# A hybrid attention block on one core: smaller spinning matmuls, and the first value weights' second half on another queue

## The chip, the cores and the metric

The kernel runs on one core of a Trainium2 chip. The metric is the device time of one execution in microseconds (us), lower is better. The core's engines are TensorE (PE in the profile; PEld are its weight loads), VectorE (DVE), ScalarE (ACT), GpSimd (POOL) and SyncE (SP). Each engine runs its instructions in the order in which they were written for it and waits for others at semaphores. Transfers between main memory and the on-chip buffers are DMAs; SP, ACT and POOL can issue them, each on a queue of its own.

## The reference: what is computed

One encoder layer over 1024 tokens of width 1024. A combined projection gives queries, keys, values and gates for two groups of heads; both groups attend, are gated with SiLU, are joined and projected, and a LayerNorm follows the residual:

```python
h = jnp.einsum('bsd,de->bse', x, w_in[layer])
q_a, k_a, v_a, z_a, q_b, k_b, v_b, z_b = jnp.split(h, SPLIT_POINTS, axis=-1)
y_a = neighborhood_attention(q_a, k_a, v_a, rel_pos_bias[layer])      # 8 heads, 8 x 16 window on a 16 x 64 grid
y_b = windowed_gqa_with_sink(rotary(q_b), rotary(k_b), v_b, sink)     # 8 query heads, 2 key heads, |i - j| <= 128
mixed = jnp.concatenate([y_a * jax.nn.silu(z_a), y_b * jax.nn.silu(z_b)], axis=-1)
x = layer_norm(DEEPNORM_ALPHA * x + jnp.einsum('bse,ed->bsd', mixed, w_out[layer]), ln_gain, ln_bias)
```

(The reshapes into heads are left out.) Inputs and output are float32.

## The kernel before, in words

Matrix products are made more precise by splitting each operand into a high and a low part and running three passes: high by high, low by high, high by low. The kernel has four stages.

1. *Values.* The 640 value columns of both groups (512 and 128) are computed first. The contraction over 1024 is cut into 8 pieces, k = 0 to 7. For the first 512 tokens, each k gives 24 matmuls of 320 columns (line 430): 4 token tiles, 2 halves of the columns, 3 passes, accumulated in 8 banks. For k = 0 alone the passes are the outer loop, so that 4 matmuls need only the first 320 columns of the weights (`wvh`, high part), the next 4 the second 320, then 8 need the low part of x and 8 the low part of the weights (`wvl`). From k = 1 on all three passes run for one tile before the next. Then the second 512 tokens follow, bank by bank.
2. *Projections* of the other columns (line 356, tiles `xf`, `wh`, `wl`) in float16, of which 15 are woven into stage 3. Before them the absolute maxima of x (`x_max`, line 439, on DVE) are gathered, turned by a TensorE transpose in `x_scale` (line 453, with the identity matrix that GpSimd makes at the start) and used to scale x.
3. *Attention* in units of 128 queries: scores (lines 709, 710), minimum and exponential, transposes by DMA, weighted values (line 774).
4. *Output projection* (line 899) and LayerNorm.

From stage 1 on the order on every engine is written out by hand (`tc.manual_schedule()`), so that the program's order decides. Loading a piece of weights (`load_wv`) is a DMA into a rotating buffer `wvraw` (3 of them), a cast on ACT for the high part (line 414) and a subtraction on DVE for the low part (line 417). x is loaded likewise into `xraw` (`load_x`, 4 buffers), with the cast on ACT, for k = 0 on DVE in two halves (line 398), and the subtraction on DVE (line 401). For k = 0 both loads are cut in two: of the weights, the first half goes out on SP, the second on GpSimd; of x, the first half goes out on ACT, the second on SP. The DMAs for k = 1 and k = 2 follow on SP.

Ahead of this stand five matmuls (line 390) on a tile of zeros, `warm`, which DVE fills (line 387). Their result isn't used. DVE fills another constant, `ones` (line 113), before that; it is read by `w_scale` (line 208), in the second half of stage 1.

Of the kernel before, what the change touches and what calls it, by code (L numbers as in the profile page):

```python
# [9 lines left out]
F16 = mybir.dt.float16  # L10
# [45 lines left out]
def hybrid_block(ctx, tc, xT, x, wt, wv, wo, bias, sink, gain, lbias, cos, sin, bmask, out):  # L56
    nc = tc.nc
# [10 lines left out]
    def bank(tag):  # L68
        bufs = {"pj": 2, "s": 4, "t": 2}[tag]
        return (ps1 if bufs == 1 else ps2).tile([128, 512], F32, tag=tag, name=f"ps_{tag}", bufs=bufs)  # L70
# [39 lines left out]
    rsg = const.tile([128, 1], F32, name="rsg")  # L110
    junk = zp.tile([128, 2048], BF16, tag="ze", name="junk", bufs=1)
    ones = const.tile([128, 128], BF16, name="ones")
    nc.vector.memset(ones, 2.0 ** -13)
    bm = const.tile([128, 384], F32, name="bm")
    sk = const.tile([128, 8], F32, name="sk")
    nsk = const.tile([128, 8], F32, name="nsk")
# [265 lines left out]
    with ExitStack() as vctx:  # L382
        vp = vctx.enter_context(tc.tile_pool(name="vp", bufs=2))
        vw = vctx.enter_context(tc.tile_pool(name="vw", bufs=1))
        wvh, wvl = [], []
        warm = vp.tile([128, 512], F16, name="warm", bufs=1)
        nc.vector.memset(warm, 0.0)
        ps = bank("t")
        for _ in range(5):
            nc.tensor.matmul(ps, warm[:, :128], warm, start=True, stop=True)  # L390

        def load_x(half, k, cuts=(0, 512)):
            raw = vp.tile([128, 512], F32, tag="xr", name="xraw", bufs=4)
# [9 lines left out]

        def load_wv(k, cuts=(0, 640)):
            raw = vp.tile([128, 640], F32, tag="wvr", name="wvraw", bufs=3)
            for q, a, b in zip((nc.sync, nc.gpsimd), cuts, cuts[1:]):
                q.dma_start(raw[:, a:b], wv[k, :, a:b])
                yield
            h = vw.tile([128, 640], F32R, name=f"wvh{k}")
            l = vw.tile([128, 640], F32R, name=f"wvl{k}")  # L410
            wvh.append(h)
            wvl.append(l)
            for a, b in zip(cuts, cuts[1:]):
                nc.scalar.copy(h[:, a:b], raw[:, a:b])
                yield
            for a, b in zip(cuts, cuts[1:]):
                nc.vector.tensor_sub(l[:, a:b], raw[:, a:b], h[:, a:b].bitcast(F32))
                yield
# [75 lines left out]
        banks = [bank(t) for t in tags]  # L494
        ordered.enter_context(tc.manual_schedule())
        first = load_wv(0, (0, 320, 640)), load_x(0, 0, (0, 256, 512))
        for i in (0, 1, 1):
            next(first[i])
        interleave(*first)
        interleave(load_wv(1), load_x(0, 1))  # L500
        for k in range(KT):
            if k + 2 < KT:
                interleave(load_wv(k + 2), load_x(0, k + 2))
            if k >= X1AT:
                interleave(load_x(1, 2 * (k - X1AT)))
                interleave(load_x(1, 2 * (k - X1AT) + 1))
                x_max(0, k - X1AT)
            for ps in ([0], [1], [2]) if k == 0 else ([0, 1, 2],):
                for a in range(2):
                    for t in range(4):  # L510
                        v_mms(banks[2 * t + a], t, a, k, ps)
# [16 lines left out]
        for i in range(8):  # L528
# [5 lines left out]
            ps = bank(tags[i])  # L534
# [503 lines left out]
    for i in range(-LD, NU + LO):  # L1038
# [29 lines left out]
        q, m = divmod(i - LP - 3, 4)  # L1068
        if i >= Q30 + 2:
            q, m = (NU // 4 - 2, i - Q30 - 2) if i < Q30 + 4 else divmod(i - LP - 3, 4)  # L1070
        elif i >= Q30:
            q, m = -1, 0
# [99 lines left out]
```

## Time and profile before

| | |
|---|---|
| median of 3 timed runs | 458.9 us (458.0 to 458.96) |
| span of the profiled execution, first to last instruction | 457.0 us |
| PE busy | 445.1 us, 97% of the span |
| DVE, ACT, POOL busy | 333.6, 287.8, 228.4 us |

The profile is one execution. Its page gives the span and no time of its own beside it; the runs' median is 1.9 us longer than the span. Views used below: the page; the list of waits (engine, line, who was waited for, us in total, times, longest); busy time by stage; the timeline (start, length, engine, line, operation, out<-in, and in brackets the idle time of the engine before it and what ended it); the chain of work that ended last (start, length, what); and the landing times of DMAs.

### The profile page before, as it was taken

The numbers are of one execution on the slowest core, as the hardware profiler recorded it, in microseconds if no ns is written. First come the engines' busy times: TensorE is split into PE (matmuls) and PEld (weight loads), VectorE is DVE, ScalarE is ACT, GpSimd is POOL, SyncE is SP. The second block draws the span as 40 slices with busy tenths as digits, with TensorE's granted clock in tenths as the row PEclk, the third lists the DMA queues.
The fourth block names the chain that finished last, engine by engine and source line by source line (L and its number), as shares of the span: only waits on it lengthen the run. The fifth ranks groups of instructions, "written<-read, shape, count | busy, mean of one in ns | idle before, by whom it ended". The sixth has DMA issues, their size and how long they took to land.

```text
span 457.0 us, 9394 instructions
## 1 busy us (share of the span) xinstructions
PE 445.1 (97%) x3238; PEld 295.3 (65%) x3238; DVE 333.6 (73%) x808; ACT 287.8 (63%) x664; POOL 228.4 (50%) x236
## 2 busy tenths in 40 slices
PE   7999999999999999999999999999999999999993
PEld 5999984444445555555555656555556788888882
DVE  4884967608988787797888887877868739099644
ACT  4627838878478878787868887786878824012100
POOL 1001953574948658688416766544663445007621
PEclk9999999999999999999999999999999999999997
DMA  7895457986658698598978979889989877004511
GB/s 222 304 309 219 139 191 270 263 300 224 227 89 182 134 190 141 127 157 151 173 130 186 177 162 224 156 191 207 191 192 225 166 224 295 0 14 149 187 58 54
DMA packets 134319, 82.28 MB, mean 180 GB/s; under 512 B 101344, under 2 KB 113376, under 8 KB 134016
## 3 DMA queue, kind: packets, MB, share of 16 engines
q1 hardware_dynamic: 133936, 81.26, 72.2%
q8 instruction: 25, 0.41, 0.4%
q0 software_dynamic: 48, 0.16, 0.2%
q10 hardware_dynamic: 288, 0.26, 0.2%
q14 instruction: 22, 0.18, 0.1%
HBM read 51.25 MB, written 9.96 MB: 134 GB/s over the span
## 4 chain that ended last, share of the span: by engine, by line
PE 91%; DVE 3%; issue 2%; ACT 2%; DMA 1%; DVEq 0%; POOL 0%; POOLq 0%; ACTq 0%
PE ps_pj L356 44%; PE ps_s L899 9%; PE ps_t L774 6%; PE ps_s L430 6%; PE ps_pj L899 6%; PE ps_t L899 5%; PE ps_s L709 4%; PE ps_s L710 4%; PE ps_pj L430 3%; PE ps_t L430 3%; PE ps_t L794 1%; DMA wvraw<-in_wv 1%; DVE qs L241 1%; ACT split L745 1%; DVE split L746 1%
## 5 line engine op out<-in xcount | busy, mean ns | idle before, releaser
L356 PE MATMUL ps_pj<-xf,wh 128*128 128x512 f16 x672 | 202.2, 379 | 0.9 <-DVE qs L241 0.6
L356 PE MATMUL ps_pj<-xf,wl 128*128 128x512 f16 x336 | 127.3, 379 | 0.0
L356 PEld LDWEIGHTS <-wh 128*128 128x128 f16 x672 | 63.5, 98 | 61.6 <-DVE ks L241 1.0
L735 ACT ACTIVATE ps_s<-sn,nm 128x385 f32<-128x385 f32 (+3 forms) x128 | 70.3, 549 | 33.0 <-DVE nm L719 31.8
L746 DVE SCALAR_TENSOR_TENSOR split<-ps_s,split 128x384 f16<-128x384 f32 (+2 forms) x128 | 65.6, 513 | 27.5 <-ACT split L745 26.1
L745 ACT ACTIVATE split<-ps_s 128x384 f16<-128x384 f32 (+2 forms) x128 | 57.4, 449 | 1.8
L356 PEld LDWEIGHTS <-wl 128*128 128x128 f16 x336 | 32.9, 98 | 37.4
L719 DVE CUSTOM_DVE_ANT_0 sn<-ps_s,bm,nsk 128x384 f32<-128x384 f32 (+1 forms) x64 | 40.8, 638 | 6.9 <-PE ps_s L710 6.4
L899 PE MATMUL ps_s<-wo,m 128*128 128x512 f32 (+1 forms) x192 | 43.3, 379 | 0.0
L719 DVE CUSTOM_DVE_ANT_0 sn<-ps_s,bias,sg 128x264 f32<-128x264 f32 (+1 forms) x64 | 35.0, 547 | 10.9 <-PE ps_s L710 4.7
L187 POOL TENSOR_SCALAR wr<-wr,wsc 128x512 f32<-128x512 f32 x26 | 20.6, 793 | 39.9 <-ACT wh L182 33.8
L709 PE MATMUL ps_s<-ks,qs 128*128 128x384 f16 (+4 forms) x128 | 39.3, 307 | 0.0
L710 PE MATMUL ps_s<-ks,qs 128*128 128x384 f16 (+4 forms) x128 | 39.2, 306 | 0.0
L899 PEld LDWEIGHTS ps_s<-wo,m 128*128 128x128 f32 x192 | 34.4, 188 | 7.0
L681 POOL TENSOR_SCALAR bias<-bias,rsg 128x552 f32<-128x552 f32 (+1 forms) x24 | 19.2, 799 | 38.0 <-DMA bias<-in_bias 34.5
L774 PEld LDWEIGHTS <-tr 128*128 128x128 f16 (+1 forms) x1104 | 36.5, 98 | 2.2 <-issue 0.3
L953 ACT ACTIVATE sd<-mv,eps 128x1 f32<-128x1 f32 x8 | 2.4, 296 | 50.5 <-DVE mv L951 46.5
L188 POOL TENSOR_TENSOR wl<-wr,wh 128x512 f16<-128x512 f32 x26 | 32.6, 1255 | 2.2
L273 POOL COPY ks<-ks 64x512 f16<-64x512 f16 x40 | 26.3, 665 | 10.3 <-DVE ks L241 5.4
L430 PE MATMUL ps_s<-wvh,x 128*128 128x320 f32 x128 | 30.8, 320 | 0.0
L989 POOL TENSOR_TENSOR xr<-xr,gb 128x512 f32<-128x512 f32 x7 | 10.3, 1475 | 40.8 <-ACT xr L986 40.8
L899 PE MATMUL ps_pj<-wo,m 128*128 128x512 f32 (+1 forms) x120 | 28.6, 376 | 0.0
(148 smaller groups left out, 830.0 us busy)
## 6 DMA issues: line engine op xcount, KB each, us to landing
xraw<-in_xT SPq DMA_DIRECT2D x31, 256.0 KB, 4.2
ws<-in_wt SPq DMA_DIRECT2D x15, 512.0 KB, 5.6
wr<-in_wt SPq DMA_DIRECT2D x26, 256.0 KB, 3.2
bias<-in_bias SPq DMA_DIRECT2D x16, 276.0 KB, 3.4
wor<-in_wo SPq DMA_DIRECT2D x16, 256.0 KB, 3.5
xr<-in_x SPq DMA_DIRECT2D x8, 512.0 KB, 7.3
out<-xr SPq DMA_DIRECT2D x14, 256.0 KB, 2.0
bias<-in_bias SPq DMA_DIRECT2D x8, 368.0 KB, 4.4
```

The lines of the kernel that those rows point to most:

```text
L188: nc.gpsimd.tensor_sub(l, raw, h)
L273: nc.gpsimd.tensor_copy(t[o, sl], t[a, sl])
L356: nc.tensor.matmul(ps, a[:, k % 4, :], mv, start=(k == 0 and i == 0), stop=(k == KT - 1 and i == 2))
L430: nc.tensor.matmul(ps[:, :320], lh[t // 4, k][:, ts], rh[k][:, cs], start=(k == 0 and i == 0), stop=(k == KT - 1 and i == 2))
L709: nc.tensor.matmul(ps[:, :m], q, sl[0], start=True, stop=False)
L710: nc.tensor.matmul(ps[:, :m], q, sl[1], start=False, stop=True)
L719: nc.vector.tensor_tensor_reduce(sn[:, :m], ps[:, :m], bias_t, sg[:, c:c + 1], init, op0=ALU.add, op1=ALU.min, accum_out=nm)
L735: nc.scalar.activation(pt[:, :m], sn[:, :m], AF.Exp, bias=nm, scale=-1.0, accum_out=sm[:, k:k + 1])
L745: nc.scalar.activation(hl[:, :m, 0, :c], src, AF.Copy, scale=PSCALE)
L746: nc.vector.scalar_tensor_tensor(hl[:, :m, 1, :c], src, PSCALE, hl[:, :m, 0, :c], op0=ALU.mult, op1=ALU.subtract)
L774: nc.tensor.matmul(ps[:, HD * m:HD * m + HD], a, b_, start=(i == 0), stop=(i == len(mms) - 1))
L899: nc.tensor.matmul(ps, lh[:, ts], rh[:, cs], start=(e == EO[0] and i == 0), stop=(e == EO[-1] and i == 2))
```

## The change

The spinning matmuls become 27 of 128 columns instead of 5 of 512, the tile `warm` shrinks from 512 to 128 columns, and its fill comes ahead of that of `ones`. The second half of the first value weights is issued by ACT, behind its load of x, and not by GpSimd. `load_wv` uses its second queue only for k = 0, where the load is cut in two. The order of the other instructions on each engine stays as it was.

```diff
     junk = zp.tile([128, 2048], BF16, tag="ze", name="junk", bufs=1)
     ones = const.tile([128, 128], BF16, name="ones")
-    nc.vector.memset(ones, 2.0 ** -13)
...
-        warm = vp.tile([128, 512], F16, name="warm", bufs=1)
+        warm = vp.tile([128, 128], F16, name="warm", bufs=1)
         nc.vector.memset(warm, 0.0)
         ps = bank("t")
-        for _ in range(5):
-            nc.tensor.matmul(ps, warm[:, :128], warm, start=True, stop=True)
+        for _ in range(27):
+            nc.tensor.matmul(ps[:, :128], warm, warm, start=True, stop=True)
+        nc.vector.memset(ones, 2.0 ** -13)
...
         def load_wv(k, cuts=(0, 640)):
             raw = vp.tile([128, 640], F32, tag="wvr", name="wvraw", bufs=3)
-            for q, a, b in zip((nc.sync, nc.gpsimd), cuts, cuts[1:]):
+            for q, a, b in zip((nc.sync, nc.scalar), cuts, cuts[1:]):
                 q.dma_start(raw[:, a:b], wv[k, :, a:b])
                 yield
```

## The prediction

> **What bounds the kernel now.** I read the page first (busy times, the chain of work that ended last), then the list of what TensorE waited for, then busy time by stage, and last the timelines of the first 12 us.
>
> ```profile
> span 457.0 us, 9394 instructions
> PE 445.1 (97%) x3238; PEld 295.3 (65%) x3238; DVE 333.6 (73%) x808; ACT 287.8 (63%) x664; POOL 228.4 (50%) x236
> PE 91%; DVE 3%; issue 2%; ACT 2%; DMA 1%; DVEq 0%; POOL 0%; POOLq 0%; ACTq 0%
> ```
>
> TensorE is busy 97% of the span and 91% of the chain is its work. Busy time by stage (columns: length, then busy time and instructions of PE, PEld, DVE, ACT, POOL, then granted clock, DMA share, GB/s) and its waits show where the other 12 us lie:
>
> ```profile
> 4.07:11.96 7.89, 6.56 (x25) 6.16 (x25) 5.07 (x10) 4.32 (x7) 0.00 (x0) 1.00 0.87 278
> 5.50:6.80 1.30, 0.00 (x0) 0.00 (x0) 0.02 (x1) 0.46 (x1) 0.00 (x0) 1.00 1.00 347
> 36.60:446.06 409.46, 408.56 (x3019) 261.07 (x3018) 301.23 (x752) 269.33 (x633) 225.46 (x227) 1.00 0.74 174
> PE ps_pj L430 <- ACT wvh L414: 1.3, 1, 1.3
> PE ps_pj L356 <- DVE qs L241: 0.6, 1, 0.6
> PE ps_pj L430 <- DVE x L398: 0.4, 1, 0.4
> ```
>
> From 36.60 to 446.06 TensorE idles 0.90 us of 409.46. So a microsecond taken from TensorE's first block is a microsecond off the end, unless another engine then becomes late. The first block itself, 24 matmuls (line 430, k = 0) from 4.07 to 11.96, is not dense:
>
> ```profile
> 1.34 2.31 PE L390 MATMUL ps_t<-warm 128*128 128x512 f16 x5 [1.34 <-DVE warm L387]
> 4.07 0.61 PE L430 MATMUL ps_pj<-wvh,x 128*128 128x320 f32 x1 [0.41 <-DVE x L398]
> ...
> 5.00 0.47 PE L430 MATMUL ps_s<-wvh,x 128*128 128x320 f32 x1
> 6.80 0.63 PE L430 MATMUL ps_pj<-wvh,x 128*128 128x320 f32 x1 [1.33 <-ACT wvh L414]
> 7.23 0.47 PE L430 MATMUL ps_s<-wvh,x 128*128 128x320 f32 x1
> 7.50 0.47 PE L430 MATMUL ps_t<-wvh,x 128*128 128x320 f32 x1
> ...
> 11.50 0.33 PE L430 MATMUL ps_s<-wvl,x 128*128 128x320 f32 x1
> 11.67 0.31 PE L430 MATMUL ps_t<-wvl,x 128*128 128x320 f32 x1
> 11.81 0.31 PE L430 MATMUL ps_s<-wvl,x 128*128 128x320 f32 x1
> 11.96 0.46 PE L430 MATMUL ps_pj<-wvh,x 128*128 128x320 f32 x2
> ```
>
> Starts lie 0.27 us apart before 11.50 (7.23 to 7.50) and 0.147 us after it (7 blocks of 24 matmuls fill the 24.64 us from 11.96 to 36.60). The same instruction runs at two speeds, although the granted clock says 1.00 throughout; the pitch is the thing to read. The 7.89 us are 1.20 for four matmuls at the long pitch (to 5.27), 1.53 idle until 6.80, 4.70 for 17 more at the long pitch (to 11.50), 0.46 for three at the short pitch. All 24 at the short pitch would be 3.53, so 4.36 us is loss. The short pitch came 4.70 us after the start of the last unbroken stretch, and the idle time stands before that stretch.
>
> Who is late is told by the timelines of the other engines, and by the landings (size, then us from issue to landing):
>
> ```profile
> 1.30 0.74 POOL L407 DMA_DIRECT2D wvraw<-in_wv  x1 [0.35 <-issue]
> 0.74 0.41 ACTq L395 DMA_DIRECT2D xraw<-in_xT  x1
> 1.19 1.28 ACT L414 ACT_TABLE_LOAD   x1 [1.19 <-PEq L1161]
> 3.44 0.46 ACT L414 CAST wvh<-wvraw 128x320 fp32r<-128x320 f32 x1 [0.97 <-DMA wvraw<-in_wv]
> 6.29 1.28 ACT L414 CAST wvh<-wvraw 128x320 fp32r<-128x320 f32 x2 [2.40 <-DMA wvraw<-in_wv]
> 7.65 0.62 ACT L398 CAST x<-xraw 128x512 fp32r<-128x512 f32 x1
> 0.84 0.17 DVE L113 MEMSET ones<- 128x128 bf16 x1 [0.84 <-PEq L1161]
> 1.01 0.27 DVE L387 MEMSET warm<- 128x256 uint32 x1
> 3.63 0.59 DVE L398 CAST x<-xraw 128x256 fp32r<-128x256 f32 x2 [2.34 <-DMA xraw<-in_xT]
> 7.60 0.83 DVE L417 TENSOR_TENSOR wvl<-wvraw,wvh 128x640 fp32r<-128x640 f32 x1 [0.33 <-ACT wvh L414]
> 8.34 0.68 DVE L401 TENSOR_TENSOR x<-xraw,x 128x512 fp32r<-128x512 f32 x1
> wvraw<-in_wv POOLq DMA_DIRECT2D x1, 160.0 KB, 5.0
> xraw<-in_xT ACTq DMA_DIRECT2D x1, 128.0 KB, 2.9
> xraw<-in_xT SPq DMA_DIRECT2D x1, 128.0 KB, 2.7
> xraw<-in_xT SPq DMA_DIRECT2D x1, 256.0 KB, 5.5
> ```
>
> The second half of the first value weights, issued by GpSimd at 1.30, lands 5.0 us later; ACT casts it at 6.29, and TensorE goes on at 6.80.
>
> **The change, part by part.**
>
> *The load on ScalarE's queue.* It is issued behind ACT's one earlier load, at about 1.17, for 0.41 us. Its landing time has two bounds: 2.9 us, the load just ahead of it in that queue, and 5.0 us, the same bytes before. I take 2.9 (same queue, nearly the same size and moment): it lands near 4.1, and with 0.46 for the cast the weights are there at 4.6, before the fifth matmul can start at 5.27. Term: the idle 1.53 goes. What it pushes: the table load moves by 0.41 and ends near 2.88, hidden by ACT's 0.97 us wait before 3.44 (without that cover 0.41 would be paid). SP's order is untouched; its fourth value-weight load, which waits for this buffer, goes out earlier, behind everything k = 1 needs. GpSimd loses 0.74 us of issuing and makes its identity matrix earlier; nobody wants that before x_scale, below.
>
> *The spins.* The fill of the smaller tile takes between 0.10 (a quarter of the columns that took 0.27, with something fixed added) and 0.17 (the row of ones), and stands first: TensorE starts near 1.05 instead of 1.34. The later fill of ones costs nothing: DVE sits idle 2.34 us before 3.63. A 128-column spin is bounded below by its columns and above by a weight load that is not overlapped:
>
> ```profile
> 1.74 0.15 PEld L390 LDWEIGHTS <-warm 128*128 128x128 f16 x1 [0.28 <-issue]
> 142.09 0.96 PE ps_t L774 x33
> ```
>
> Five 512-column spins ran from 1.34 to 3.65 at about 0.43 us a start (the weight load has 0.15 of work and 0.28 idle), so 128 columns are 0.107; with 0.15 in series they would be 0.257. I take 0.107, because 33 matmuls of line 774, each with its own weight load, pass in 0.96 us. So 27 end at 1.05 + 2.89 = 3.94. The first real matmul waits for DVE's cast as before and starts at 4.07: no delay, and a hole of about 0.1 us.
>
> *The short pitch.* If the spins count as part of the unbroken stretch, it comes at 1.05 + 4.70 = 5.75; if only real matmuls count, at 4.07 + 4.70 = 8.77. In the first case the block runs 1.68 us at the long pitch (six matmuls), then 18 at 0.147: it ends at 8.4. In the second it ends at 4.07 + 4.70 + 7 x 0.147 = 9.80. The Trainium skill (TensorE: Matmul & The Clock Gate, Part 1) says that the clock gate opens after a busy window of about 3.4 us which runs free of the kernel's start. By it the opening would fall between 4.5 and 7.9 here, an estimate, and the saving between 2.6 and 2.9 us from run to run; the trace's 4.70 us fits such a window, but one trace can't show the freedom.
>
> *What is late next.* For k = 1 the ACT cast of x began at 7.65, as its load landed (256 KB, 5.5 us from an issue near 2.1), and DVE finished the low part at 8.34 + 0.68 = 9.02. These loads stand in one stream: the DMA share is 1.00 at 347 GB/s from 5.50 to 6.80, and the change takes no bytes away. So I leave k = 1's operands at 9.02, and the block of k = 1 starts at about 9.05 instead of 11.96.
>
> *Later cover.* x_scale needs the maxima of all x, which are a DVE matter:
>
> ```profile
> 36.70 0.17 DVE L527 TENSOR_REDUCE gm<-xm 128x1 f32<-128x16 f32 x1
> 41.75 0.29 DVE L454 TENSOR_REDUCE gm<-ps_t 128x1 f32<-128x128 f32 x1 [4.88 <-PE ps_t L453]
> ```
>
> They are ready at 36.87, and DVE then waits 4.88 us for TensorE. A TensorE that is 2.9 us earlier still comes 2 us after them. All later orders are unchanged and triggered by TensorE's progress.
>
> *Sum.* 11.96 - 9.05 = 2.91 us off the profiled span: 457.0 becomes 454.1. The median of the timed runs is 458.9, 1.9 above that span; with the same difference I forecast 456.0. Ends for the unknowns: 2.16 (long pitch until 8.77) and 3.5 (k = 1's operands not late, block ends at 8.4); the three runs (458.0 to 458.96) add half a microsecond each way.
>
> **The rivals.**
>
> *Spins don't count towards the short pitch.* The zeros keep the array busy but the short pitch comes 4.70 us after 4.07: 2.16 us saved, 456.7. For it: in before the spins at 1.34 to 3.65 opened nothing. Against: holes of 0.41 and 1.33 us followed them.
>
> *The load comes no sooner.* If it queues behind the bytes of the other loads, only the issue is gained: 0.13 in start and 0.33 in length, 0.46 us. Then TensorE resumes at 6.34 and everything else repeats: 458.4, no change. For it: the stream is full at 347 GB/s. Against: the 160 KB would be issued ahead of the 256 KB load near 2.1, and its neighbours with 128 KB landed in 2.7 and 2.9 us. The Trainium skill (DMA: Bandwidth & Descriptors, Issuing engines are not separate DMA queues) states this rival's rule: all queues share the same 16 engines, so another issuer saves only issue time. The rows 5.0 against 2.9 speak against it here, though sizes and moments differ a little.
>
> *Slower: spins paced by their weight loads.* With 0.257 each they last until 1.05 + 6.94 = 7.99, in order ahead of the real work, and the array streams in only 42% of that, so the short pitch must be earned again: 4.70 + 7 x 0.147 = 5.73 more, k = 1 at 13.7, 460.7. It loses from the point where the real work starts after 11.96 - 5.73 = 6.23, a pitch of 0.19 us. Against: the row of line 774.
>
> *Swallowed later.* If x's maxima or a later DVE step came due, the gain would shrink to within the measurement; against it stand the 4.88 us and the 0.90 us of idle time.
>
> **How the numbers follow.** Forecast (2.3 to 3.6 us off): 0.60. Spins don't count: 0.17. Load no sooner: 0.10. Slower by pacing: 0.08. Swallowed: 0.05. A measurement of this kernel tells about 0.2%, 0.9 us. The first two are faster (0.77), load and swallowed are the same (0.15), the rest slower (0.08). The range: forecast with the runs' spread from 454.9, up to 458.1, which takes in the second case and part of the third.
>
> **What would show it.** Right: spins end near 3.95; the second cast of wvh on ACT starts near 4.1; no idle of TensorE between 4.07 and the end of k = 0; the pitch drops to 0.147 well before 8; k = 1 starts near 9 with a short wait for DVE's low part of x; idle after 36 us as now. Wrong: a wait for wvraw near 6, a first real matmul after 4.5, the long pitch beyond 9, or new TensorE waits behind x_scale.

## The result, and the profile after

The changed kernel takes 455.41 us (median of 10 runs, 455.14 to 457.45), the kernel before 457.76 us (10 runs, 456.22 to 458.96). The ratio is 0.9955 with a 95% interval of 0.9937 to 0.9973: 1.2 to 2.9 us, 2.06 at the centre; the two medians differ by 2.35 us. Forecast were 456.0 us and a range of 454.9 to 458.1. The profiled span fell from 457.0 to 453.4 us.

Two lines of the changed kernel's page; then, in the next fence, TensorE's timeline (start, length, line, operation, count, idle time before and what ended it):

```profile
span 453.4 us, 9438 instructions
...
PE 443.6 (98%) x3260; PEld 295.2 (65%) x3260; DVE 333.3 (73%) x808; ACT 287.7 (63%) x664; POOL 227.7 (50%) x235
```

```profile
0.99 3.06 PE L389 MATMUL ps_t<-warm 128*128 128x128 f16 x27 [0.99 <-DVE warm L386]
4.22 0.63 PE L430 MATMUL ps_pj<-wvh,x 128*128 128x320 f32 x1 [0.17 <-ACT wvh L414]
4.66 0.47 PE L430 MATMUL ps_s<-wvh,x 128*128 128x320 f32 x1
5.11 0.49 PE L430 MATMUL ps_t<-wvh,x 128*128 128x320 f32 x1
5.44 0.31 PE L430 MATMUL ps_s<-wvh,x 128*128 128x320 f32 x1
5.58 0.31 PE L430 MATMUL ps_pj<-wvh,x 128*128 128x320 f32 x1
...
8.52 0.46 PE L430 MATMUL ps_pj<-wvh,x 128*128 128x320 f32 x2
```

The hole of 1.33 us ahead of the fifth matmul (5.58) is gone, the pitch is 0.147 us from 5.44 on, and k = 1 starts at 8.52, not at 11.96: 3.44 us. What comes after that is as long as it was: from the start of k = 1 to the end of the span it is 445.04 us before and 444.88 after.

ACT and DVE of the changed kernel show when the operands were there; the last three lines are landings (queue, size, us from issue to landing):

```profile
1.17 0.45 ACTq L407 DMA_DIRECT2D wvraw<-in_wv  x1
1.65 1.28 ACT L414 ACT_TABLE_LOAD   x1 [1.65 <-PEq L1161]
3.71 0.46 ACT L414 CAST wvh<-wvraw 128x320 fp32r<-128x320 f32 x1 [0.78 <-DMA wvraw<-in_wv]
4.53 0.46 ACT L414 CAST wvh<-wvraw 128x320 fp32r<-128x320 f32 x1 [0.36 <-DMA wvraw<-in_wv]
6.39 0.62 ACT L398 CAST x<-xraw 128x512 fp32r<-128x512 f32 x1
4.76 0.29 DVE L398 CAST x<-xraw 128x256 fp32r<-128x256 f32 x1 [0.93 <-DMA xraw<-in_xT]
7.23 0.69 DVE L401 TENSOR_TENSOR x<-xraw,x 128x512 fp32r<-128x512 f32 x1
38.30 0.29 DVE L454 TENSOR_REDUCE gm<-ps_t 128x1 f32<-128x128 f32 x1 [2.15 <-PE ps_t L453]
wvraw<-in_wv ACTq DMA_DIRECT2D x1, 160.0 KB, 3.3
xraw<-in_xT SPq DMA_DIRECT2D x1, 128.0 KB, 3.5
xraw<-in_xT SPq DMA_DIRECT2D x1, 256.0 KB, 4.2
```

The second half of the weights is cast at 4.53 instead of 6.29. In exchange x's second half, whose place on SyncE's queue did not change, came at 4.76 instead of about 3.9 (its landing took 3.5 us, not 2.7), which is why the third matmul starts 0.45 us after the second. The load of 256 KB for k = 1 took 4.2 us instead of 5.5, and the low part of x for k = 1 is done at 7.23 + 0.69 = 7.92, not at 9.02. DVE waits 2.15 us for x_scale, as forecast.

What filled the DMA engines in the meantime: busy time from 4 to 5 us (the last three columns are the granted clock, the DMA share and GB/s), first of the kernel before, then of the changed one.

```profile
4.00:5.00 1.00, 0.93 (x3) 0.96 (x4) 1.00 (x4) 0.00 (x0) 0.00 (x0) 1.00 0.80 208
```

```profile
4.00:5.00 1.00, 0.83 (x3) 0.50 (x2) 0.24 (x2) 0.63 (x2) 0.00 (x0) 1.00 0.97 365
```

The transfers had a lull before the stretch that the prediction looked at, 208 GB/s against 347 from 5.50 to 6.80. The change filled it: the three profiled executions of the changed kernel moved 365, 381 and 294 GB/s here, two of the kernel before 208 and 210.

### The profile page after: what moved, and what is told of

It reads as the page before. It is cut to its first block, busy times and chain, and to the rows that moved or that the text cites. A ratio compares the mean times of both kernels' runs of the same rounds, so it can differ in the third digit from the quotient of the medians.

```text
span 453.4 us, 9438 instructions
## 1 busy us (share of the span) xinstructions
PE 443.6 (98%) x3260; PEld 295.2 (65%) x3260; DVE 333.3 (73%) x808; ACT 287.7 (63%) x664; POOL 227.7 (50%) x235
## 4 chain that ended last, share of the span: by engine, by line
PE 88%; DVE 3%; issue 2%; POOL 2%; DMA 2%; ACT 2%; DVEq 0%; SPq 0%; POOLq 0%; ACTq 0%
PE ps_pj L355 42%; PE ps_s L899 9%; PE ps_s L430 6%; PE ps_t L774 6%; PE ps_pj L899 6%; PE ps_t L899 5%; PE ps_s L709 3%; PE ps_s L710 3%; PE ps_pj L430 3%; PE ps_t L430 3%; DMA bias<-in_bias 1%; PE ps_t L794 1%; DVE qs L240 1%; POOL ks L272 1%; ACT split L745 1%
## 5 line engine op out<-in xcount | busy, mean ns | idle before, releaser
L430 PE MATMUL ps_s<-wvh,x 128*128 128x320 f32 x128 | 29.6, 311 | 0.0
```

The lines of the kernel that those rows point to most:

```text
L430: nc.tensor.matmul(ps[:, :320], lh[t // 4, k][:, ts], rh[k][:, cs], start=(k == 0 and i == 0), stop=(k == KT - 1 and i == 2))
```

## The experiments

The theory: two losses, one after the other. The load's delay made TensorE idle; and a hole in TensorE's work, wherever it stands, puts off the moment at which the pitch falls from 0.267 to 0.147 us. Rivals: only one of the two parts matters; the moment doesn't depend on TensorE's work; the queue as such doesn't matter. All edits are against the changed kernel, except where said.

**The spins alone.**

```diff
-            for q, a, b in zip((nc.sync, nc.scalar), cuts, cuts[1:]):
+            for q, a, b in zip((nc.sync, nc.gpsimd), cuts, cuts[1:]):
```

> The 27 spins and the early fill of the changed kernel, but the second half of the first value weights still issued by GpSimd. Theory (both parts are needed, and a hole after the pitch has become short does no harm): the weights land near 6.3, TensorE idles from about 5.3 to 6.8, but the pitch is 0.147 us from about 5.3 on, so k = 1 starts at 6.8 + 20 x 0.147 = 9.7, against 11.96 before and 8.52 with the whole change; 2.2 us below before on the profiled spans. Rival (the hole of 1.3 us sets the count back): the short pitch comes only 4.7 us after 6.8, k = 1 near 12, no gain.

Ratio to the kernel before 0.9977 (0.9958 to 0.9995), median 456.59 us. TensorE's timeline:

```profile
5.02 0.43 PE L430 MATMUL ps_t<-wvh,x 128*128 128x320 f32 x1
5.29 0.31 PE L430 MATMUL ps_s<-wvh,x 128*128 128x320 f32 x1
6.47 0.42 PE L430 MATMUL ps_pj<-wvh,x 128*128 128x320 f32 x1 [0.88 <-ACT wvh L414]
6.73 0.31 PE L430 MATMUL ps_s<-wvh,x 128*128 128x320 f32 x1
6.88 0.31 PE L430 MATMUL ps_t<-wvh,x 128*128 128x320 f32 x1
```

The pitch is short from about 5.1 on, the hole of 0.88 us behind that moment does not lengthen it again, and k = 1 starts at 9.52 (9.7 expected), 1.0 us later than with the whole change, because TensorE idles. By the ratios about half of the gain stays away. Single runs spread from 456.06 to 460.12, much wider than those of the changed kernel; an execution in which the hole comes before the moment would lose the most, but none of those was profiled.

**The load alone** (against the kernel before).

```diff
-            for q, a, b in zip((nc.sync, nc.gpsimd), cuts, cuts[1:]):
+            for q, a, b in zip((nc.sync, nc.scalar), cuts, cuts[1:]):
```

> The load on ScalarE's queue, but the five spins of 512 columns and the old order of the fills. Theory (the hole of 0.4 us between spins and real work sets the count back, and the short pitch needs 4.3 to 4.7 us without one): no idle in k = 0, short pitch near 8.7, k = 1 near 9.8, 2.1 us below before. Rival (a hole of 0.4 us does no harm, so the new spins are worth only their start at 0.99 instead of 1.34): short pitch near 5.7, k = 1 near 8.7, within 0.3 us of the whole change.

Ratio 0.996 (0.9945 to 0.9975), median 456.49 us.

```profile
4.20 0.64 PE L430 MATMUL ps_pj<-wvh,x 128*128 128x320 f32 x1 [0.55 <-ACT wvh L414]
...
7.96 0.45 PE L430 MATMUL ps_s<-wvh,x 128*128 128x320 f32 x1
8.22 0.34 PE L430 MATMUL ps_t<-wvh,x 128*128 128x320 f32 x1
8.40 0.31 PE L430 MATMUL ps_s<-wvh,x 128*128 128x320 f32 x1
```

No idle time after 4.20, but the pitch falls only near 8.2, 4.0 us after the first real matmul; k = 1 starts at 9.72 (9.8 expected). The five large spins did nothing here: a hole of 0.55 us followed them.

**The whole change without spins** (the loop of 27 removed).

> The whole change without any spins; this leaves out only matmuls whose result isn't used. Theory (activity from the first real matmul on counts): first real matmul at 4.2, short pitch near 8.7, k = 1 near 9.8; the spins are worth 1.2 to 1.3 us of the whole gain and the load the rest. Rival (the pitch changes at a moment of its own, not by what TensorE did before): short pitch near 5.3 as with the spins, k = 1 near 8.5, the same time as the changed kernel.

Ratio 0.9966 (0.9952 to 0.9979), median 456.74 us; first real matmul at 4.11, short pitch from about 7.9, k = 1 at 9.45. That is the load alone within 0.3 us, and the rival of a moment independent of TensorE's work, which expected the changed kernel's time, is out. In this execution 0.2 us each were waited for a DVE step and a transpose much later.

**Fewer spins** (22 instead of 27), so that they end earlier.

> The whole change with 22 spins, which end near 3.45 and leave a hole of 0.65 us or more before the first real matmul near 4.2. Theory (a hole of about half a microsecond sets the count back, a smaller one doesn't): the pitch shortens only 3.8 to 4.6 us after the first real matmul, near 8.0 to 8.8; k = 1 near 9.6 to 10.0; median 1.0 to 1.6 us above the changed kernel, close to the run without spins. Rival (the spins' start counts, holes don't matter): pitch short from about 5.3, the time of the changed kernel.

Ratio 0.9978 (0.9963 to 0.9993), median 456.96 us (12 runs), 1.56 above the changed kernel's 455.40, measured beside it.

```profile
4.22 0.63 PE L430 MATMUL ps_pj<-wvh,x 128*128 128x320 f32 x1 [0.71 <-ACT wvh L414]
...
7.56 0.42 PE L430 MATMUL ps_s<-wvh,x 128*128 128x320 f32 x1
7.82 0.31 PE L430 MATMUL ps_pj<-wvh,x 128*128 128x320 f32 x1
```

The first real matmul starts at 4.22, as in the changed kernel's profile. Five spins less leave a hole of 0.71 us, and the pitch falls at 7.8 instead of 5.3. The next two executions, with 27 spins each, show that the hole decides and not the number of spins.

**The changed kernel again, and again.**

> The changed kernel once more, unedited, for a second look at its first 10 us and for its spread beside these runs. Theory (the pitch shortens a fixed 4 to 4.6 us after TensorE's unbroken work begins): at 5.0 to 5.6 again, and the runs lie within 1 us except for single ones. Rival (the moment is free of what the kernel does): anywhere between 4.4 and 7.9.

> The changed kernel once more beside these two, for a third look. Theory: where the hole before the first real matmul is under 0.4 us in the profiled execution, the pitch is short from 5.0 to 6.2 and k = 1 starts before 9; where it is over 0.45, the pitch is long until 8 or later and k = 1 starts near 10. From the start of k = 1 to the end of the span it takes 444.9 to 445.1 us in both cases.

Medians 455.16 (6 runs) and 455.40 us (12 runs); ratios 0.9934 (0.9918 to 0.995) and 0.9954 (0.9937 to 0.9971). The first of the two profiled executions was one of the longer ones, 456.83 us:

```profile
4.52 0.63 PE L430 MATMUL ps_pj<-wvh,x 128*128 128x320 f32 x1 [0.47 <-ACT wvh L414]
...
8.75 0.42 PE L430 MATMUL ps_s<-wvh,x 128*128 128x320 f32 x1
9.01 0.31 PE L430 MATMUL ps_pj<-wvl,x 128*128 128x320 f32 x1
```

The first weights landed later, the hole behind the spins was 0.47 us, the pitch fell near 8.9 and k = 1 started at 10.18. So the rival in which the spins don't count describes some executions of this kernel. The theory of a fixed delay from the spins' start fell here. The other execution had a hole of 0.18 us and the short pitch from 4.7, a little before the expected 5.0, and shows the limit that the prediction named, in a milder form:

```profile
8.15 0.31 PE L430 MATMUL ps_pj<-wvh,x 128*128 128x320 f32 x1
8.80 0.41 PE L430 MATMUL ps_pj<-wvh,x 128*128 128x320 f32 x1 [0.35 <-DVE x L401]
```

With k = 0 done at 8.15, the second matmul of k = 1 waited for DVE's low part of x until 8.80. That is also why the expected 444.9 to 445.1 us from k = 1 to the end is 445.55 here; it is 444.92 in the first.

**The kernel before again.**

> The kernel before once more, unedited. Theory: the second half of the weights again lands between 5.8 and 6.6, and the pitch shortens 3.9 to 4.6 us after TensorE resumes. Rival (a moment free of what the kernel does): anywhere from 3.4 to 6.8 us after it resumes; the spread of 3.6 us in the times of the kernel before would come from there.

457.75 us, span 456.0. TensorE resumed at 6.11, the pitch fell near 10.0 and k = 1 started at 10.92. Two executions of the same kernel, 1.04 us apart at the start of k = 1 (11.96 and 10.92), are 1.0 us apart in span. GpSimd's load took 4.3 us here, 5.0 there, and landed near 5.6, a little before the expected 5.8. The fall came 3.9 us after TensorE resumed, 4.7 in the first profile.

**More spins** (31 instead of 27, twice).

> The whole change with 31 spins, which end near 4.4, so that no hole is left in most executions. Theory: first real matmul near 4.4 to 4.6, pitch short between 4.9 and 6.2, k = 1 between 8.3 and 8.9; median within 0.4 us of the changed kernel, and no run 1.5 us above its own lowest unless a later wait lengthens it. Rival (the runs of the changed kernel that were 1.6 to 2 us above the others have another cause): such runs come here as often.

> 31 spins once more, for the spread: 6 of 28 runs of the changed kernel were above 456.3, and none of six with 31 spins. Theory (those runs are the executions whose hole before the first real matmul set the count back): no run above 456.3 here, median 455.1 to 455.5. Rival (another cause): one or two in six above 456.3.

Medians 455.33 and 455.53 us, ratios 0.9949 (0.993 to 0.9968) and 0.9947 (0.9927 to 0.9967). The first profiled execution:

```profile
0.99 3.49 PE L389 MATMUL ps_t<-warm 128*128 128x128 f16 x31 [0.99 <-DVE warm L386]
4.29 0.63 PE L430 MATMUL ps_pj<-wvh,x 128*128 128x320 f32 x1
...
5.34 0.31 PE L430 MATMUL ps_s<-wvh,x 128*128 128x320 f32 x1
```

No hole, and the pitch fell near 5.2; in the second profiled execution, without a hole too, it fell near 6.1 and k = 1 started at 8.85. All 12 runs lie between 455.05 and 455.84 us; of 28 runs of the changed kernel, 6 lie between 456.33 and 457.45. The median is the same. That the longer runs are gone fits the theory; 12 runs are few to prove it.

**Many more spins** (45).

> The whole change with 45 spins. Theory (zeros alone shorten the pitch some 4 us after the start, and spins stand in order ahead of the real work): the pitch of the spins themselves falls from 0.113 to near 0.06 us between 4.8 and 5.4, they end near 5.6, the first real matmul starts there and all 24 run at 0.147, so k = 1 starts near 9.1, 0.6 us later than with 27. Rival (real data are needed): the spins keep 0.113 to the end at 6.1 and real matmuls begin at 0.267.

Ratio 0.9953 (0.9938 to 0.9968), median 456.0 us.

```profile
0.99 4.98 PE L389 MATMUL ps_t<-warm 128*128 128x128 f16 x45 [0.99 <-DVE warm L386]
5.73 0.61 PE L430 MATMUL ps_pj<-wvh,x 128*128 128x320 f32 x1
6.14 0.41 PE L430 MATMUL ps_s<-wvh,x 128*128 128x320 f32 x1
6.39 0.31 PE L430 MATMUL ps_t<-wvh,x 128*128 128x320 f32 x1
PE ps_t L774 <- DMA tr<-split: 1.2, 1, 1.2
```

The spins held their long pitch to the end (45 in 4.74 us, 0.105 each) and the short pitch came near 6.2, 5.2 us after the start, so the expected 4.8 to 5.4 was wrong; real matmuls waited behind the spins until 5.73 and k = 1 until 9.62. The last row, from the list of TensorE's waits, is a single wait for a transpose in the attention stage, another 1.2 us; of the other executions only the one without spins waited there, for 0.2 us. Whether it came by chance or by the shift stays open. This execution was the longest of the ten, 457.88 us.

**The second half on SyncE's queue**, as its third load.

```diff
-            for q, a, b in zip((nc.sync, nc.scalar), cuts, cuts[1:]):
+            for q, a, b in zip((nc.sync, nc.sync), cuts, cuts[1:]):
```

> The whole change, but the second half of the weights is the third load on SyncE's queue instead of the second on ScalarE's. Theory (what was late was GpSimd's issue and its descriptors, any of the two other queues will do, since the bytes ahead are the same): the half lands between 4.3 and 5.0, in time for the fifth matmul, k = 1's loads land within 0.4 us of the changed kernel's, and the time is that of the changed kernel within 0.5 us. Rival (ScalarE's queue is worth something by itself, as a second queue beside SyncE's): the half lands behind the other SyncE loads, past 5.5, and TensorE idles before the fifth matmul for 0.7 us or more.

Ratio 0.9976 (0.996 to 0.9991), median 457.37 us. TensorE, ACT's cast and the landing of the half, then the DMA rate from 4 to 5 us:

```profile
4.97 0.30 PE L430 MATMUL ps_s<-wvh,x 128*128 128x320 f32 x1
6.40 0.41 PE L430 MATMUL ps_pj<-wvh,x 128*128 128x320 f32 x1 [1.13 <-ACT wvh L414]
5.89 0.46 ACT L414 CAST wvh<-wvraw 128x320 fp32r<-128x320 f32 x1 [1.98 <-DMA wvraw<-in_wv]
wvraw<-in_wv SPq DMA_DIRECT2D x1, 160.0 KB, 4.2
```

```profile
4.00:5.00 1.00, 0.95 (x5) 0.93 (x4) 1.00 (x4) 0.00 (x0) 0.00 (x0) 1.00 0.50 77
```

My theory fell and the rival held. GpSimd is gone, and still the half lands near 5.9 and TensorE idles 1.13 us. The lull is deeper than before, 77 GB/s. The ratio is that of the run with the load on GpSimd (0.9977). So taking the load off GpSimd gains nothing by itself; its new place has to be early enough. The profiled execution was a short one, 456.13 us against the median of 457.37; what the longer ones lost besides isn't shown.

**The second halves exchanged**: x's on ScalarE, the weights' as SyncE's second load.

```diff
-            for q, a, b in zip((nc.scalar, nc.sync) if len(cuts) == 3 else (nc.sync,), cuts, cuts[1:]):
+            for q, a, b in zip((nc.scalar, nc.scalar) if len(cuts) == 3 else (nc.sync,), cuts, cuts[1:]):
...
-            for q, a, b in zip((nc.sync, nc.scalar), cuts, cuts[1:]):
+            for q, a, b in zip((nc.sync, nc.sync), cuts, cuts[1:]):
```

> The whole change with the two second halves exchanged: ScalarE's queue carries both halves of the first x tile, SyncE's both halves of the first value weights. Theory (what helps is a second queue with more than one load on it, whichever load it is): DMA moves over 330 GB/s between 4 and 5 us, the second half of the weights lands before 5, x's second half before 4.5 instead of 4.7, and the time is that of the changed kernel within 0.5 us. Rival (the 160 KB must be on ScalarE's queue): under 230 GB/s between 4 and 5 us, as in the run with the load on SyncE, and an idle TensorE of 0.7 us or more ahead of the fifth matmul; 1 us or more above the changed kernel.

Ratio 0.994 (0.9923 to 0.9957), median 455.31 us, like the changed kernel.

```profile
4.56 0.46 ACT L414 CAST wvh<-wvraw 128x320 fp32r<-128x320 f32 x1 [0.19 <-DMA wvraw<-in_wv]
4.24 0.29 DVE L398 CAST x<-xraw 128x256 fp32r<-128x256 f32 x1 [0.22 <-DMA xraw<-in_xT]
```

It does not matter which load is the second on ScalarE's queue: both halves are there when they are needed. The rate from 4 to 5 us was 230 GB/s, where I expected over 330. So two loads on each queue bring the first tiles in time, but the lull as such, and its cause, stay open.

## Why the prediction was right, and where it was not

- *TensorE is the bound, and the first block is where the gain lies.* Right: what follows the start of k = 1 took 444.85 to 445.08 us in 10 of 14 profiled executions. The other four were 0.6 to 1.4 us longer, the third profile of the changed kernel by the wait for DVE shown above, three runs with edits partly by single later waits (a transpose, a weight's low part).
- *The load.* Right in kind. I took 2.9 us to the landing, it was 3.3, and the idle time was gone all the same. "SP's order is untouched" was true, but not harmless: x's second half, on that queue, took 3.5 us instead of 2.7 (3.0 to 3.6 in all nine executions with the weights' half on ScalarE's queue, 2.7 or 2.8 in the four with it on GpSimd's or as SyncE's third).
- *The spins.* The pitch of 0.107 us was right: 22, 27, 31 and 45 spins last 2.53, 3.06, 3.49 and 4.98 us, about 0.106 for each one more. The sum left out that the last spin goes on for some 0.2 us beyond one pitch, so the 27 ended at 4.05, not at 3.94. They leave a hole of 0.17 us before 4.22, where I had 0.1 before 4.07; the first real matmul waited for ACT's cast of the weights, not for DVE's cast of x as I had written. The rival of 0.257 per spin, with its loss, did not occur. The short pitch came at 5.3 (forecast 5.75) in the first profile, at 4.7 in the third, at 8.9 in the second, so the fixed 4.70 us from the start of the work was wrong. I had put "spins count" and "spins don't count" as two possible worlds; they are two outcomes of one kernel, and the hole behind the spins decides between them.
- *What is late next.* This step failed: k = 1's operands were at 7.92 us, not at 9.02, and k = 0 ended at 8.52, near the 8.4 that I had worked out for the block by itself. I took a stretch with a DMA share of 1.00 for the whole stream, and so overlooked the lull just before it. With 9.02 I forecast 2.91 us off the span; it was 3.6. Not all of the 1.1 us is the change: the operands were there at 7.92 to 8.90 in the ten executions in which the half came early (8.3 in the middle), and at 8.50 to 9.17 in the four in which it came late (8.9), about half a microsecond between them.
- *The base.* I set the sum against 458.9, the median of three runs. Over ten it is 457.76, and the profiled execution of before was one of the longer ones (span 457.0, a second one 456.0). That error and the last have opposite signs: the gain between the two profiles was larger than forecast, the gain between the medians smaller (2.35 us against 2.9), and 456.0 came out 0.6 us too high. So it is partly luck that 456.0 came so close. The base itself wavers: in the two later sets of runs the kernel before had medians of 458.43 us (17 runs) and 458.34 us (23 runs), and the changed kernel beside it was 3.27 and 2.94 us faster.
- *Sum of the parts.* Both parts alone are worth about 0.23% and 0.4% by their ratios, the whole 0.45% to 0.66% in three sets of runs. Spins without the load leave TensorE idle; the load without spins leaves the pitch long for four microseconds. The spins' own worth, given the load, is the distance to 22 spins: 1.56 us between the medians, 0.24% or 1.1 us by the ratios.

## What to carry to other kernels

Read the start of a kernel by the pitch of equal matmuls, not by the granted clock, which said 1.00 on both sides of the fall. Spins help only if they reach the first real matmul: here a hole of 0.7 us behind them cost 1.56 us, and four spins more, at no loss in the median, kept 12 of 12 runs below 455.9. And read the landing of each first load, on every queue that could issue it: the same half landed in time as the second load on ScalarE's or SyncE's queue, and too late as SyncE's third and as the first on GpSimd's. The place in line counts, but it does not tell everything.

## What the runs showed of the hardware

Pitch. With TensorE busy from 0.99 us on, the pitch fell at 4.7 to 6.2 us, 3.7 to 5.2 after the start; where a hole stood before the real matmuls, 3.6 to 4.7 us after TensorE had resumed. Zeros count: with the spins, and no harmful hole behind them, the pitch fell 0.5 to 1.6 us after the first real matmul, without them 3.8. But it never fell while only spins ran, 4.74 us of them in the longest case, so that zeros alone would do isn't shown. Holes of 0.17 to 0.38 us behind the spins did no harm, those of 0.47 to 0.71 did, and once the pitch was short 0.9 and 1.1 us did none. Whether the single hole counts or all idle time of some stretch, these runs don't tell apart. The Trainium skill (TensorE: Matmul & The Clock Gate, Part 1) has a free-running window of about 3.4 us that must be busy. All 14 executions are compatible with that: no fall came earlier than 3.4 us after the work began, and with 31 spins and no hole it came at two moments, near 5.2 and near 6.1. That a window with a small hole still counts is not in what I cite of the Trainium skill; here a hole of 0.38 us did and one of 0.47 did not.

Queues. The same 160 KB took 5.0, 4.6 and 4.3 us on GpSimd's queue, 4.2 as SyncE's third load and 3.0 to 3.3 as the second load of ScalarE or SyncE. The Trainium skill (DMA: Bandwidth & Descriptors, Issuing engines are not separate DMA queues) says that another issuer saves only issue time. Moving this load from ScalarE's second place to SyncE's third delayed its issue by about half a microsecond and its cast by 1.36 us (4.53 to 5.89). The measurement decides: here the place in a queue was worth more than the issue. Why GpSimd's queue was slow with no load ahead of it isn't shown.
